# Three experts ranked by comparison, router work of a mixer tile in two slots, the next expert picked one step later, and weights split through a queue: an encoder block on one core

## The chip, the cores and the metric

The kernel runs on one core of a Trainium2 chip. The metric is the device time of one execution in microseconds, as the median of three runs. The engines of the core are TensorE (PE: matmuls and transposes), VectorE (DVE), ScalarE (ACT), GpSimd (POOL) and SyncE (SP, which here only issues transfers). Each works through its own queue in order, and semaphores make one wait for another.

## The reference

One layer of an encoder on 1024 tokens of width 1024, in float32: a token mixer and then a mixture of experts in which each expert picks its tokens.

```python
p = jnp.einsum('bsd,dk->bsk', modulate(rms_norm(x, g_norm_mix), shift_m, scale_m), w_in)
z = gate_a * (fourier_mix(u_f) @ w_fourier) + gate_b * ((b_g * centred_conv3(c_g * v)) @ w_conv_out)
x = x + gate_m * (z @ w_o)
h = modulate(rms_norm(x, g_norm_moe), shift_f, scale_f)
# expert_choice_moe(h), 16 experts, cap = 2 * 1024 / 16 = 128 tokens each
probs = softmax(h @ w_router + b_router)
vals, idx = lax.top_k(jnp.swapaxes(probs, 1, 2), cap)      # per expert: its 128 tokens
xe = h[idx]
a, u = xe @ w_gate_e, xe @ w_up_e                          # 1024 -> 2048, per expert
y = (silu(a) * u) @ w_down_e                               # 2048 -> 1024
x = x + gate_f * scatter_add(y * vals)
return rms_norm(x, g_final)
```

## The kernel before

**The stages.** A mixer (0 to about 757 us), whose last part, `mix_out`, goes over eight tiles of 128 tokens: z @ w_o, the residual, the norm, the router's logits and its softmax. Then the router's end and the first gather (to about 777 us), then the 16 experts one after the other (to about 1930 us), and the last expert's rows, which leave by a scattered transfer.

**Precision.** Weights and activations are float32. Each is split into a high and a low part: ACT copies the high part (rounded) and DVE subtracts it (`split`, L92 and L93). A product is then three matmuls: high x high, high x low and low x high. For a weight matrix of an expert the parts are called whi and wlo; for the expert's tokens xh and xl; for the product h = silu(a) * u, transposed, hth and htl.

**An expert.** Its weights are 24 units of 1 MB, each two halves of 1024 columns. A half costs ACT one copy (whi), DVE one subtraction (wlo) and PE six matmuls of 512 columns. Six buffers of whi and six of wlo are there (`NWB`), and a ring of twelve units of raw weights ahead of them, which SP fills. The 2048 inner columns go in four parts, fc 0 to 3, of 512. For each part `expert` computes a (four halves), u (four halves) and, for the part before, y (four halves). `put(fc)` transposes h of a part with four PE transposes (L1205), and ACT and DVE make hth and htl of them. During fc 1, `pick` finds the next expert's tokens: DVE compares each token's place with the slots (oh, L1068), PE multiplies it by the table (L1075), DVE reads r, idx and val from that, and POOL gathers the rows (xg). `turn` transposes xg at the end of the expert (L1104). The expert's result is scaled into ys (L1269) and added to the tokens in memory; the code puts this addition off into the next expert (`self.left`).

**The last expert** has some of its halves multiplied without a split (`plain`, L1222, with htf, the unsplit transposed h), while ACT and DVE norm the finished rows of the other tokens (`final`, `FIN` says where they are loaded).

**Choosing tokens.** An expert takes the 128 tokens with the highest probability. For experts 0 and 1 (`NCMP` = 2), `compare` ranks the tokens during `mix_out`: DVE compares each token's probability with that of all tokens of earlier tiles (cmp) and of its own tile (own), and PE counts (L972). For the other 14, `router` searches the threshold in steps during the first experts (mask, cand, ok, base).

**Order.** A scheduler orders each engine's queue from the order in which the code is written, from priorities and from dependencies. `issue_after` pins one instruction behind another. Within `mix_out`, `side(n)` puts the previous tile's router work ahead of k-step n of the present tile's eight.

Of the kernel before, what the change touches and what calls it, by code (L numbers as in the profile page):

```python
# [15 lines left out]
P = 128  # L16
D = 1024
# [12 lines left out]
NCMP = 2  # L30
FIN = ((10, 0), (8, 2), (6, 4), (4, 6))
# [49 lines left out]
class Block:  # L81
# [578 lines left out]
    def rstd(self, pool, ss, name):  # L660
        nc = self.nc
        n = ss.shape[1]
        ms = pool.tile([P, n], F32, name=name + "ms")
        nc.vector.tensor_scalar(ms, ss, 1.0 / D, EPS, op0=OP.mult, op1=OP.add)
        rs = pool.tile([P, n], F32, name=name + "rs", bufs=2)
        nc.gpsimd.tensor_tensor(rs, ms, self.neghalf[:, 0:n], op=OP.pow)
        return rs
# [66 lines left out]
    def mix_out(self, pool):  # L734
# [91 lines left out]
        def side(n):  # L826

            t, x2, rs = prev
            if t == 0 and n in (1, 5):
                next(rw, None)  # L830
            if n == 1 and t:
                hold["cmp"] = self.compare(t - 1, range(NCMP), psum)
                next(hold["cmp"])
            if n == 3:
                if t:
                    next(hold["cmp"], None)
                hold["xt"] = turned()
                for hf in range(2):
                    turn(x2, hold["xt"], hf)
            if n == 6:  # L840
                pl = psum()
                for hf in range(2):
                    logits(pl, hold["xt"], hf)
                softmax(t, rs, pl)

        prev, hold = None, {}
        for t in range(ST):
# [37 lines left out]
            for n in range(2):  # L885
                cs = slice(512 * n, 512 * n + 512)
                for k in range(KD):
                    s = {(0, 1): 1, (0, 4): 3, (1, 0): 6}.get((n, k))
                    if s:
                        side(s)  # L890
                    if n == 1 and k == 4:
# [43 lines left out]
    def compare(self, t, es, psum):  # L935
# [12 lines left out]
        num = pc[:, 256:256 + 8 * ne].rearrange("p (e t) -> p e t", e=ne)  # L948
# [12 lines left out]
        for i, e in enumerate(es):  # L961
            own = pool.tile([P, P], BF16, name="own", bufs=2)
# [3 lines left out]
            if last:  # L966
                own = pool.tile([P, P], BF16, name="own", bufs=2)
# [87 lines left out]
    def route_rest(self, pool):  # L1055
        yield from self.compare(ST - 1, (1,), self.psum)
# [82 lines left out]
    def plain(self, rows):  # L1139

        raw = self.take().rearrange("p (i k n) -> p i k n", i=2, k=rows // 2)
        for i in range(2):
            yield raw[:, i]
            if i:
                self.fetch()
            self.step()

    def unit(self, rows):

        raw = self.take()  # L1150
        nc = self.nc
        for i in range(2):
            hi = self.wsp.tile([P, 1024], F32R, name="whi")
            lo = self.wsp.tile([P, 1024], F32R, name="wlo")
            src = raw[:, 1024 * i:1024 * i + 1024]
# [7 lines left out]
            else:  # L1163
                self.split(hi, lo, src)
            self.npop += 1
            if i:
                if self.npop <= NWS:
                    with self.tc.issue_after(self.gather):
                        self.fetch(nc.gpsimd)
                else:  # L1170
                    self.fetch()
            self.pin = self.last
            self.step()
            yield hi.rearrange("p (k n) -> p k n", k=rows // 2), lo.rearrange("p (k n) -> p k n", k=rows // 2)

    def expert(self, pool, e, picked, side):
# [8 lines left out]
        def up(fc, name):  # L1185
            ps = self.pau.tile([P, 512], F32, name=name)
            k = 0
            for b in range(2):
                for j, (wh, wl) in enumerate(self.unit(4)):
                    if self.npop > NWB and (j == 0 or self.ranked < 2):  # L1190
# [5 lines left out]
                if self.left:  # L1196
                    self.left.pop()()
            return ps

        def put(fc):  # L1200
# [6 lines left out]
            if last and fc in (1, 2):  # L1207
                hf = pool.tile([P, 4, P], F32, name="htf")
# [9 lines left out]
        def down(fc, b):  # L1218
            if last and (fc, b) in ((1, 1), (2, 0), (2, 1)):
                for i, w in enumerate(self.plain(2)):  # L1220
                    for n in (0, 512):
                        nc.tensor.matmul(y[:, n:n + 512], lhsT=ht[fc][2][:, 2 * b + i, :], rhs=w[:, 0, n:n + 512],  # L1222
                                         start=False, stop=False)
                return
            for i, (wh, wl) in enumerate(self.unit(2)):
# [7 lines left out]
        for fc in range(4):  # L1233
            pa = up(fc, "a")
            if last and fc == 0:
# [28 lines left out]
        if not last:  # L1264
            down(3, 1)

            def add():
                ys = pool.tile([P, D], F32, name="ys")
                nc.vector.scalar_tensor_tensor(ys, in0=y, scalar=val, in1=self.gf, op0=OP.mult, op1=OP.mult)  # L1269
                nc.gpsimd.indirect_dma_start(out=self.x2_d,  # L1270
                                             out_offset=bass.IndirectOffsetOnAxis(ap=idx[:, 0:1], axis=0),
                                             in_=ys, in_offset=None, compute_op=OP.add)
                self.scattered = e == NE - 2

            self.left.append(add)
            return nxt
        w = list(self.unit(2))
        for _ in range(8):
            self.step()
        ss = pool.tile([P, 3], F32, name="sse")  # L1280
        for n, cs in enumerate((slice(0, 512), slice(512, 768), slice(768, 1024))):
# [4 lines left out]
            nc.vector.scalar_tensor_tensor(h, in0=y[:, cs], scalar=val, in1=self.gf[:, cs], op0=OP.mult, op1=OP.mult)  # L1286
            nc.vector.tensor_tensor(xg[:, cs], xg[:, cs], h, op=OP.add)
# [36 lines left out]
    def run(self):  # L1324
# [94 lines left out]
        self.nfetch, self.npop, self.units, self.rows = 0, 0, [], []  # L1419
        def last():  # L1420
# [80 lines left out]
```

## Time and profile before

| | us |
|---|---|
| Median of 3 runs (lowest, highest) | 1948.76 (1948.51, 1949.74) |
| The profiled execution | 1944.46 |
| Its span in the trace | 1942.6 |
| PE busy (share of the span) | 1888.7 (97%) |
| DVE busy | 1583.4 (82%) |
| ACT busy | 1117.6 (58%) |

The profile is of one execution, whose time is 1.86 us more than its span, and lies 4.3 us under the median of the runs. A share of busy time says which engine the kernel cannot do without, and not where its gaps are: PE at 97% leaves some 54 us without a matmul in the whole kernel, some 15 of them in the first 50 us, 14 after 1926 us, and 13 in the steady experts between 920 and 1926 us. Transfers move 283 GB/s in the mean and are not the limit in the experts: SP's queue waits 875 us there for a buffer that DVE has yet to finish with.

### The profile page before, as it was taken

The numbers are of one execution on the slowest core, as the hardware profiler recorded it, in microseconds if no ns is written. First come the engines' busy times: TensorE is split into PE (matmuls) and PEld (weight loads), VectorE is DVE, ScalarE is ACT, GpSimd is POOL, SyncE is SP. The second block draws the span as 40 slices with busy tenths as digits, with TensorE's granted clock in tenths as the row PEclk, the third lists the DMA queues.
The fourth block names the chain that finished last, engine by engine and source line by source line (L and its number), as shares of the span: only waits on it lengthen the run. The fifth ranks groups of instructions, "written<-read, shape, count | busy, mean of one in ns | idle before, by whom it ended". The sixth has DMA issues, their size and how long they took to land.

```text
span 1942.6 us, 23945 instructions
## 1 busy us (share of the span) xinstructions
PE 1888.7 (97%) x8777; PEld 1507.7 (78%) x8777; DVE 1583.4 (82%) x2005; ACT 1117.6 (58%) x1403; POOL 136.2 (7%) x124
## 2 busy tenths in 40 slices
PE   6999999999999999999999999999999999999996
PEld 5788888777788877777888777777778778777873
DVE  5976678676853767999999898898998999989886
ACT  5533233433510433776787777777767777677764
POOL 1000000000130111000000000000000000000001
PEclk9999999999999999999999999999999999999998
DMA  8322224465774842999999999999999999999993
GB/s 298 128 67 65 87 76 154 143 228 195 232 250 140 291 180 108 396 367 346 378 372 389 354 359 376 372 364 360 392 364 355 386 366 361 380 373 355 392 367 135
DMA packets 244746, 549.02 MB, mean 283 GB/s; under 512 B 12644, under 2 KB 51652, under 8 KB 244628
## 3 DMA queue, kind: packets, MB, share of 16 engines
q1 hardware_dynamic: 229248, 494.50, 69.8%
q0 software_dynamic: 14528, 52.75, 8.6%
q8 instruction: 69, 1.13, 0.2%
q10 hardware_dynamic: 852, 0.24, 0.1%
q14 instruction: 49, 0.40, 0.1%
HBM read 507.61 MB, written 39.86 MB: 282 GB/s over the span
## 4 chain that ended last, share of the span: by engine, by line
PE 76%; DVE 12%; DMA 5%; issue 4%; ACT 2%; POOL 0%; ACTq 0%; POOLq 0%; DVEq 0%
PE pb L315 9%; DVE wlo L93 7%; PE pa L315 6%; PE pc L315 6%; PE u L1302 5%; PE u L1300 5%; PE u L1301 5%; PE y L106 5%; PE y L109 4%; PE y L112 4%; PE a L1302 4%; PE a L1301 4%; PE a L1300 4%; DMA raw<-in_w_up_e_dram 3%; PE mm L106 3%
## 5 line engine op out<-in xcount | busy, mean ns | idle before, releaser
L93 DVE TENSOR_TENSOR wlo<-raw,whi 128x1024 fp32r<-128x1024 f32 x759 | 889.0, 1218 | 61.1 <-ACT whi L92 52.5
L92 ACT ACTIVATE whi<-raw 128x1024 fp32r<-128x1024 f32 x759 | 751.4, 1052 | 61.2 <-PE y L112 21.6
L1302 PE MATMUL a<-wlo,xh 128*128 128x512 f32 x512 | 206.2, 403 | 7.0 <-DVE wlo L93 5.7
L1302 PE MATMUL u<-wlo,xh 128*128 128x512 f32 x512 | 203.6, 398 | 2.4 <-DVE wlo L93 2.4
L1300 PE MATMUL u<-whi,xh 128*128 128x512 f32 x512 | 202.5, 395 | 1.6 <-ACT whi L92 1.6
L1300 PE MATMUL a<-whi,xh 128*128 128x512 f32 x512 | 201.5, 394 | 1.9 <-ACT whi L92 1.6
L1301 PE MATMUL a<-whi,xl 128*128 128x512 f32 x512 | 201.8, 394 | 0.0
L1301 PE MATMUL u<-whi,xl 128*128 128x512 f32 x512 | 201.8, 394 | 0.0
L109 PE MATMUL y<-wlo,hth 128*128 128x512 f32 x496 | 161.3, 406 | 0.5 <-DVE wlo L93 0.3
L106 PE MATMUL y<-whi,hth 128*128 128x512 f32 x496 | 159.5, 402 | 0.0
L112 PE MATMUL y<-whi,htl 128*128 128x512 f32 x496 | 156.4, 396 | 0.0
L92 ACT ACTIVATE wh<-s 128x512 fp32r<-128x512 f32 x80 | 50.3, 631 | 135.9 <-PE pc L315 76.0
L1302 PEld LDWEIGHTS a<-wlo,xh 128*128 128x128 f32 x512 | 96.4, 188 | 39.3 <-DVE wlo L93 19.8
L1302 PEld LDWEIGHTS u<-wlo,xh 128*128 128x128 f32 x512 | 96.3, 188 | 31.1 <-DVE wlo L93 8.0
L1300 PEld LDWEIGHTS a<-whi,xh 128*128 128x128 f32 x512 | 96.7, 189 | 21.9 <-ACT whi L92 2.5
L1301 PEld LDWEIGHTS a<-whi,xl 128*128 128x128 f32 x512 | 96.5, 188 | 22.0 <-DVE xl L93 0.4
L1300 PEld LDWEIGHTS u<-whi,xh 128*128 128x128 f32 x512 | 96.5, 188 | 21.0 <-ACT whi L92 2.6
L1301 PEld LDWEIGHTS u<-whi,xl 128*128 128x128 f32 x512 | 96.6, 189 | 20.5
L112 PEld LDWEIGHTS y<-whi,htl 128*128 128x128 f32 x496 | 93.4, 189 | 22.5
L106 PEld LDWEIGHTS y<-whi,hth 128*128 128x128 f32 x496 | 91.8, 189 | 20.9 <-issue 0.5
L109 PEld LDWEIGHTS y<-wlo,hth 128*128 128x128 f32 x496 | 89.9, 190 | 20.4 <-DVE wlo L93 2.4
L1243 ACT ACTIVATE h<-a 128x512 f32<-128x512 f32 x64 | 38.2, 596 | 106.6 <-PE a L1302 106.6
(530 smaller groups left out, 3183.1 us busy)
## 6 DMA issues: line engine op xcount, KB each, us to landing
raw<-in_w_gate_e_dram SPq DMA_DIRECT2D x126, 1024.0 KB, 7.2
raw<-in_w_up_e_dram SPq DMA_DIRECT2D x126, 1024.0 KB, 9.1
raw<-in_w_down_e_dram SPq DMA_DIRECT2D x126, 1024.0 KB, 8.1
ld<-in_w_ada_dram SPq DMA_DIRECT2D x48, 512.0 KB, 5.4
ld<-in_w_in_dram SPq DMA_DIRECT2D x44, 512.0 KB, 4.4
sg_d<-q POOLq DMA_DIRECT2D x8, 1024.0 KB, 6.1
ld<-sg_d SPq DMA_DIRECT2D x16, 512.0 KB, 4.9
x<-in_x_dram SPq DMA_DIRECT2D x8, 512.0 KB, 3.3
```

Of the source, the lines that this page charges most:

```text
L92: a = self.nc.scalar.activation(hi, src, AF.Copy).ins
L93: self.last = a, self.nc.vector.tensor_tensor(lo, src, hi, op=OP.subtract).ins
L106: nc.tensor.matmul(o, lhsT=lh, rhs=rh, start=first, stop=False)
L109: nc.tensor.matmul(o, lhsT=lh, rhs=rl, start=False, stop=False)
L112: nc.tensor.matmul(o, lhsT=ll, rhs=rh, start=False, stop=last)
L315: nc.tensor.matmul(o, lhsT=x[:, k, :], rhs=y[:, k, :], start=first and k == 0 and i == 0, stop=last and k == 3 and i == 2, skip_group_chec ...
L1243: nc.scalar.activation(h, pa, AF.Silu)
L1300: nc.tensor.matmul(o, lhsT=lhs[0], rhs=rhs[0], start=first, stop=False, **kw)
L1301: nc.tensor.matmul(o, lhsT=lhs[1], rhs=rhs[0], start=False, stop=False, **kw)
L1302: nc.tensor.matmul(o, lhsT=lhs[0], rhs=rhs[1], start=False, stop=last, **kw)
```

## The change

It does seven things. (1) `NCMP` is 3: one more expert is ranked by comparison, the search is for 13 experts. (2) The router work of a mixer tile is issued at two k-steps, 2 and 6, instead of 1, 3 and 6 (for tile 0 at 1, 3, 5 and 6), and the counting half of `compare` follows the softmax; in the last tile the places change likewise. (3) The next expert is picked in fc 2 (`PICK`) and no longer in fc 1. (4) Weight halves go through a queue: `half` issues the split of one half, and `unit` fills the queue up to six halves before it hands one to the matmuls. The order in which units come is written in a list, `plan`; `free` asks for the next transfer. (5) silu(a) is issued right behind a, and ys right behind the expert's last part. (6) htf has two buffers, and the final rows are loaded at other places (`FIN`). (7) At the end one multiplication by the final gain stands behind the first operation of `rstd`, with the order pinned.

```diff
-NCMP = 2
-FIN = ((10, 0), (8, 2), (6, 4), (4, 6))
+NCMP = 3
+PICK = 2
+FIN = ((8, 0), (7, 2), (5, 4), (4, 6))
+PLAIN = ((1, 1), (2, 0), (2, 1))
...
-            if t == 0 and n in (1, 5):
-                next(rw, None)
-            if n == 1 and t:
-                hold["cmp"] = self.compare(t - 1, range(NCMP), psum)
-                next(hold["cmp"])
-            if n == 3:
-                if t:
-                    next(hold["cmp"], None)
+            if n == 2:
+                if t == 0:
+                    next(rw, None)
                 hold["xt"] = turned()
                 for hf in range(2):
                     turn(x2, hold["xt"], hf)
+                if t:
+                    hold["cmp"] = self.compare(t - 1, range(NCMP), psum)
+                    next(hold["cmp"])
             if n == 6:
...
                 softmax(t, rs, pl)
+                if t:
+                    next(hold["cmp"], None)
...
-                    s = {(0, 1): 1, (0, 4): 3, (1, 0): 6}.get((n, k))
+                    s = {(0, 4): 2, (1, 1): 6}.get((n, k))
...
+        self.queue.append([x.rearrange("p (k n) -> p k n", k=rows // 2) for x in parts])
...
+    def unit(self):
+
+        for i in range(2):
+            while len(self.queue) < NWB and self.nunit < len(self.plan):
+                self.half()
+            self.nused += 1
+            yield self.queue.pop(0)
...
-                hf = pool.tile([P, 4, P], F32, name="htf")
+                hf = pool.tile([P, 4, P], F32, name="htf", bufs=2)
...
             pa = up(fc, "a")
+            h = pool.tile([P, 512], F32, name="h", bufs=2)
+            nc.scalar.activation(h, pa, AF.Silu)
...
             pu = up(fc, "u")
-            h = pool.tile([P, 512], F32, name="h", bufs=2)
-            nc.scalar.activation(h, pa, AF.Silu)
             nc.vector.tensor_tensor(h, pu, h, op=OP.mult)
             hs[fc] = h
-            if fc == 1:
+            if fc == PICK:
...
-            nc.vector.tensor_tensor(xg[:, cs], xg[:, cs], self.gl[:, cs], op=OP.mult)
+            if n < 2:
+                with tc.issue_after(order):
+                    order = nc.vector.tensor_tensor(xg[:, cs], xg[:, cs], self.gl[:, cs], op=OP.mult).ins
...
-        rs = self.rstd(pool, st, "e")
+        rs, order = self.rstd(pool, st, "e", True)
+        with tc.issue_after(order):
+            nc.vector.tensor_tensor(xg[:, cs], xg[:, cs], self.gl[:, cs], op=OP.mult)
```

What the scheduler makes of it is seen in the engines' queues. Line numbers of the changed program differ: its split is L94 and L95, its put L1222.

PE's queue where u of fc 2 ends in an expert in the middle of the run, before:

```order
L1302 MATMUL u<-wlo,xh 128x512
L106 MATMUL y<-whi,hth 128x512 x2
L109 MATMUL y<-wlo,hth 128x512 x2
L112 MATMUL y<-whi,htl 128x512 x2
L106 MATMUL y<-whi,hth 128x512 x2
L1205 MATMUL tp<-ident,h 128x128 x4
```

and of the change, at the same place:

```order
L1323 MATMUL u<-wlo,xh 128x512
L108 MATMUL y<-whi,hth 128x512 x2
L111 MATMUL y<-wlo,hth 128x512 x2
L114 MATMUL y<-whi,htl 128x512 x2
L108 MATMUL y<-whi,hth 128x512 x2
L111 MATMUL y<-wlo,hth 128x512 x2
L114 MATMUL y<-whi,htl 128x512 x2
L108 MATMUL y<-whi,hth 128x512 x2
L1222 MATMUL tp<-ident,h 128x128 x4
```

The four transposes of h have moved from 8 to 14 matmuls behind the end of u. ACT's queue in the same expert, from the h of fc 0 to the hth of fc 2, before:

```order
L1243 ACTIVATE h<-a 128x512
L92 ACTIVATE whi<-raw 128x1024 x6
L92 ACTIVATE hth<-tp 128x512
L92 ACTIVATE whi<-raw 128x1024 x2
L1243 ACTIVATE h<-a 128x512
L92 ACTIVATE whi<-raw 128x1024 x8
L92 ACTIVATE hth<-tp 128x512
L92 ACTIVATE whi<-raw 128x1024 x4
L1243 ACTIVATE h<-a 128x512
L92 ACTIVATE whi<-raw 128x1024 x6
L92 ACTIVATE hth<-tp 128x512
```

and of the change:

```order
L1254 ACTIVATE h<-a 128x512
L94 ACTIVATE whi<-raw 128x1024 x6
L94 ACTIVATE hth<-tp 128x512
L94 ACTIVATE whi<-raw 128x1024 x2
L1254 ACTIVATE h<-a 128x512
L94 ACTIVATE whi<-raw 128x1024 x6
L94 ACTIVATE hth<-tp 128x512
L94 ACTIVATE whi<-raw 128x1024 x6
L1254 ACTIVATE h<-a 128x512
L94 ACTIVATE whi<-raw 128x1024 x6
L94 ACTIVATE hth<-tp 128x512
```

The hth of fc 1 (the second of the three) now has six copies ahead of it, as the others have, and had eight. In the tail, PE's queue where u of fc 2 of the last expert ends, before:

```order
L1302 MATMUL u<-wlo,xh 128x512
L1205 MATMUL tp<-ident,h 128x128 x4
L106 MATMUL y<-whi,hth 128x512 x2
L109 MATMUL y<-wlo,hth 128x512 x2
L112 MATMUL y<-whi,htl 128x512 x2
L106 MATMUL y<-whi,hth 128x512 x2
L109 MATMUL y<-wlo,hth 128x512 x2
L112 MATMUL y<-whi,htl 128x512 x2
L1222 MATMUL y<-raw,htf 128x512 x4
L1300 MATMUL a<-whi,xh 128x512
```

and of the change:

```order
L1323 MATMUL u<-wlo,xh 128x512
L108 MATMUL y<-whi,hth 128x512 x2
L111 MATMUL y<-wlo,hth 128x512 x2
L114 MATMUL y<-whi,htl 128x512 x2
L108 MATMUL y<-whi,hth 128x512 x2
L111 MATMUL y<-wlo,hth 128x512 x2
L114 MATMUL y<-whi,htl 128x512 x2
L1239 MATMUL y<-raw,htf 128x512 x4
L1222 MATMUL tp<-ident,h 128x128 x4
L1321 MATMUL a<-whi,xh 128x512
```

The transposes stand behind the matmuls without a split (L1222 before, L1239 in the change) and no longer ahead of the part y.

## Rows read from the trace of the kernel before

Times of the timeline are from the start of the span: start, duration, engine, line, operation, tiles, count; in brackets what the engine waited before it.

**Rows 1.** The page's groups by line: engine, tiles, count, busy, mean ns, idle before.

```profile
L93 DVE TENSOR_TENSOR wlo<-raw,whi 128x1024 fp32r<-128x1024 f32 x759 | 889.0, 1218 | 61.1 <-ACT whi L92 52.5
L92 ACT ACTIVATE whi<-raw 128x1024 fp32r<-128x1024 f32 x759 | 751.4, 1052 | 61.2 <-PE y L112 21.6
```

**Rows 2.** Busy time by stretches: length, PE, PEld, DVE, ACT, POOL, PEclk, DMA, GB/s.

```profile
777.00:895.00 118.00, 115.41 (x622) 89.59 (x621) 115.50 (x185) 87.74 (x91) 3.71 (x2) 1.00 1.02 380
880.00:900.00 20.00, 17.16 (x85) 12.91 (x84) 19.93 (x36) 11.19 (x12) 1.13 (x1) 0.87 0.94 351
920.00:1926.00 1006.00, 992.61 (x4486) 790.60 (x4485) 902.21 (x884) 731.22 (x825) 55.92 (x33) 1.00 1.00 365
...
1340.00:1360.00 20.00, 19.57 (x90) 15.55 (x89) 18.30 (x18) 14.65 (x18) 2.32 (x1) 1.00 0.97 322
1898.00:1902.00 4.00, 3.90 (x11) 2.60 (x10) 3.59 (x5) 3.23 (x5) 0.31 (x1) 0.57 0.87 351
```

**Rows 3.** Timeline of PE behind ys in expert 8.

```profile
1353.19 0.39 PE L1301 MATMUL a<-whi,xl 128*128 128x512 f32 x1
1354.01 0.50 PE L1302 MATMUL a<-wlo,xh 128*128 128x512 f32 x1 [0.43 <-DVE wlo L93]
```

**Rows 4.** Timeline of PE and DVE at the pick in expert 8.

```profile
1368.35 0.36 PE L1075 MATMUL tp<-v,oh 128*128 128x5 bf16 x8
...
1371.18 0.40 PE L1301 MATMUL u<-whi,xl 128*128 128x512 f32 x1
1371.75 0.50 PE L1302 MATMUL u<-wlo,xh 128*128 128x512 f32 x1 [0.18 <-DVE wlo L93]
...
1369.02 0.15 DVE L1077 COPY r<-tp 128x5 f32<-128x5 f32 x1
...
1370.48 2.35 DVE L93 TENSOR_TENSOR wlo<-raw,whi 128x1024 fp32r<-128x1024 f32 x2
```

**Rows 5.** Timeline of PE, ACT and DVE at two hth in expert 8.

```profile
1363.77 0.60 PE L1205 MATMUL tp<-ident,h 128*128 128x128 f32 x4
...
1364.40 0.60 ACT L92 ACTIVATE hth<-tp 128x512 fp32r<-128x512 f32 x1 [1.50 <-PE tp L1205]
...
1380.56 0.27 PE L1205 MATMUL tp<-ident,h 128*128 128x128 f32 x1
...
1383.20 0.40 PE L1301 MATMUL a<-whi,xl 128*128 128x512 f32 x1
1383.72 0.51 PE L1302 MATMUL a<-wlo,xh 128*128 128x512 f32 x1
...
1380.87 0.60 ACT L92 ACTIVATE hth<-tp 128x512 fp32r<-128x512 f32 x1 [4.60 <-PE tp L1205]
1381.36 2.94 ACT L92 ACTIVATE whi<-raw 128x1024 fp32r<-128x1024 f32 x3
...
1382.44 2.36 DVE L93 TENSOR_TENSOR wlo<-raw,whi 128x1024 fp32r<-128x1024 f32 x2 [0.25 <-ACT whi L92]
```

**Rows 6.** PE's waits in the whole span: total us, times, longest.

```profile
PE sm L972 <- DVE cmp L958: 2.5, 6, 0.6
```

**Rows 7.** Timeline of DVE at the end of the mixer's last tile.

```profile
755.63 1.14 DVE L958 TENSOR_SCALAR_CACHE_REDUCE cmp<-prow,prob 128x896 bf16<-128x896 f32 x1
...
757.63 0.69 DVE L804 TENSOR_TENSOR ld<-mm,ld 128x512 f32<-128x512 f32 x1
```

**Rows 8.** Timeline of PE at the pick of expert 2.

```profile
895.75 0.38 PE L1075 MATMUL tp<-v,oh 128*128 128x5 bf16 x8 [2.85 <-DVE oh L1068]
```

**Rows 9.** Timeline of ACT and PE in the last expert.

```profile
1894.77 0.60 ACT L1209 ACTIVATE htf<-tp 128x512 f32<-128x512 f32 x1 [7.00 <-PE y L1222]
...
1896.36 0.50 PE L1300 MATMUL a<-whi,xh 128*128 128x512 f32 x1 [1.63 <-ACT whi L92]
...
1906.43 0.50 PE L1300 MATMUL u<-whi,xh 128*128 128x512 f32 x1 [1.63 <-ACT whi L92]
```

**Rows 10.** Timeline of DVE behind the last y.

```profile
1931.99 0.42 DVE L1289 TENSOR_TENSOR xg<-xg,ys 128x256 f32<-128x256 f32 x1 [0.63 <-ACT h L1288]
```

More of the change, by code (lines that the diff above doesn't have):

```diff
@@ L961, in compare @@
         for i, e in enumerate(es):
-            own = pool.tile([P, P], BF16, name="own", bufs=2)
+            own = pool.tile([P, P], BF16, name="own")
             r = row[:, i, :] if last else self.prow[:, e, n:n + P]
@@ L1055, in route_rest @@
     def route_rest(self, pool):
-        yield from self.compare(ST - 1, (1,), self.psum)
+        yield from self.compare(ST - 1, range(1, NCMP), self.psum)
         self.ranked = NCMP
@@ L1137, in step, with half @@
                 next(r, None)
[L1139 to L1150, printed above, removed]
-        nc = self.nc
-        for i in range(2):
+    def half(self):
+        nc = self.nc
+        rows, plain = self.plan[self.nunit]
+        i = self.nhalf
+        if i == 0:
+            self.raw = self.take()
+        src = self.raw[:, 1024 * i:1024 * i + 1024]
+        if plain:
+            parts = [src]
+        else:
             hi = self.wsp.tile([P, 1024], F32R, name="whi")
             lo = self.wsp.tile([P, 1024], F32R, name="wlo")
-            src = raw[:, 1024 * i:1024 * i + 1024]
+            parts = [hi, lo]
             if self.npop < NWS:
@@ L1164, in unit, with free @@
                 self.split(hi, lo, src)
+                self.pin = self.last
             self.npop += 1
[L1166 to L1174, printed above, removed]
+        self.queue.append([x.rearrange("p (k n) -> p k n", k=rows // 2) for x in parts])
+        if i:
+            if not plain:
+                self.free(self.nunit)
+            self.nunit += 1
+        self.nhalf = 1 - i
+        self.step()
+    def free(self, n):
+        self.read.add(n)
+        while self.nfree in self.read:
+            self.nfree += 1
+            if self.nfree == 1:
+                with self.tc.issue_after(self.gather):
+                    self.fetch(self.nc.gpsimd)
+            else:
+                self.fetch()
+    def unit(self):
[4 more added lines that the diff above has]
+            yield self.queue.pop(0)
     def expert(self, pool, e, picked, side):
@@ L1218, in down @@
         def down(fc, b):
-            if last and (fc, b) in ((1, 1), (2, 0), (2, 1)):
-                for i, w in enumerate(self.plain(2)):
+            if last and (fc, b) in PLAIN:
+                for i, (w,) in enumerate(self.unit()):
                     for n in (0, 512):
@@ L1419, in run @@
         self.nfetch, self.npop, self.units, self.rows = 0, 0, [], []
+        self.plan = []
+        for e in range(NE):
+            for f in range(5):
+                self.plan += [(4, False)] * (4 if f < 4 else 0)
+                self.plan += [(2, e == NE - 1 and (f - 1, b) in PLAIN) for b in range(2 if f else 0)]
+        self.nunit, self.nhalf, self.nfree, self.nused, self.queue, self.read = 0, 0, 0, 0, [], set()
         def last():
@@ L1474, in run @@
         self.hold = self.turned
-        self.left = []
         for e in range(NE):
```

45 lines of the change are left out of this document (23 added, 22 removed).

## Prediction

> **What bounds the kernel now.** I first read the busy time by stretches. TensorE (PE) is busy 992.61 of the 1006 us from 920 to 1926, at a granted clock of 1.00, while DVE has 902.21 and ACT 731.22 [rows 2]. So in the experts the time is the sum of PE's own work, and a change is worth what it adds to or takes from PE's gaps. The groups by line give the price of a half: ACT copies it to whi in 1052 ns, DVE makes wlo in 1218 ns [rows 1]; PE takes six matmuls about 0.23 us apart, 1.385 us. Both helpers are faster than PE, and there are six buffers of each, so in the mean PE need not wait. It waits where ACT or DVE has to stop for something that PE itself does late.
>
> The timelines show three such places in each of the experts 5 to 13, every 71.02 us. (1) Behind ys, a DVE instruction: starts at 1353.19 and 1354.01 where 0.23 is usual, a loss of 0.59 (11 times) [rows 3]. (2) Behind r, idx, val, oh: DVE is off the wlo from 1369.02 to 1370.48, and PE's starts are 1371.18 and 1371.75: 0.34 lost (9 times) [rows 4]. (3) Behind hth of fc 1, the place to understand [rows 5]. The last transpose starts at 1380.56; only 0.31 later can ACT copy it, at 1380.87; the next whi starts at 1381.36, its wlo at 1382.44, and PE reads that at 1383.72. PE had wanted it at 1383.20 + 0.23: lost 0.29 (9 times, and 0.63 once in expert 4). So 1.22 us per expert, about 13 in all. Note that ACT had been idle 4.60 before that hth: it stood in its queue ahead of the whi that it could have made.
>
> **Lead** is what I call the halves that ACT has issued ahead of hth, less those that PE has finished when the transposes start. At (3) it is 1.67 (h of the second matrix's a has lead 2; eight whi follow it in ACT's order; PE does four halves of u, four of y and two matmuls). For the other hth of before it is 2.67 (six whi, four halves of u and eight matmuls: 2 + 6 - 5.33), and there PE has no gap: transposes at 1363.77, hth at 1364.40, and the next matmul with wlo on time [rows 5].
>
> **Steady experts.** The new code writes the splits ahead of the matmuls that need them, and the program's order shows what this does: six whi still stand between h and hth, but the transposes come 14 matmuls behind u instead of 8. The lead becomes 2 + 6 - 6.33 = 1.67 in fc 0, 1 and 2 (2.0 in fc 3). The price follows from the rows just read. With T0 the start of four transposes: hth at T0 + 0.63 (1363.77 to 1364.40), from hth to PE 2.85 (1380.87 to 1383.72), so T0 + 3.48. PE wants it after the transposes (0.35), ten matmuls of finished halves and two that need whi only: 0.35 + 12 x 0.23 = T0 + 3.10, or 3.14 in y. Loss 0.38 and 0.34 at fc 0 and fc 2, where before has none.
>
> At fc 1 the pick of the next expert now stands two wlo behind that htl, where before it stood behind the htl of fc 0. Two wlo start at T0 + 2.20 and end their turn at T0 + 4.50 (2 x 1.15), r to oh takes 1.46 [rows 4], to T0 + 5.96, and the next wlo reaches PE 1.28 later (1382.44 to 1383.72), T0 + 7.24. PE wants it four halves on: 0.35 + 5.54 + 0.12, and 0.22 for the eight oh matmuls (0.36 from first start to last end [rows 4], less the overlap with the next), T0 + 6.23. Loss 1.01, the hth's own part in it. The ys keeps its lead of two halves, so 0.59 stays; that ys is issued at once and not in the next expert changes nothing in DVE's order here, as wlo of the queue stand ahead of it.
>
> Per expert: 0.59 + 0.38 + 1.01 + 0.34 = 2.32 against 1.22, +1.10; ten experts (4 to 13) +11.0. Expert 14 picks nothing: about +0.8. Expert 15 loses 0.38 and 0.34 and, at fc 1, has htf and hth both ahead of the whi, about 0.5 more: +1.2. Together **+13**. Bounds: +4 if a lead of 1.67 costs nothing where the transposes fall inside y, and only the pick costs; +21 if each hth costs 0.63 as the one in expert 4 did.
>
> **Mixer.** PE waits 2.5 us in 6 places at L972 for the compare [rows 6]; from start to start the gaps there are some 4 us. The second half of compare now comes behind softmax, four k-steps later, so DVE's cmp (0.6 to 1.1 us each) is done: -4.0. The third expert adds seven transposes and 21 small matmuls on PE, +1.8 at 0.05 for each of the small ones and some 0.1 for each transpose. In the last tile DVE's order has a third cmp and own ahead of the add to ld; a cmp of 896 columns takes 1.14, and that add started at 757.63 with PE idle for it [rows 7]. The two cost 1.4, some 0.4 of it was slack (the place and cnt additions are moved behind): +1.0. Sum **-1.1**, bounds -2.5 and +1.
>
> **First experts.** From 777 to 895 DVE is full, 115.5 of 118 us [rows 2]: it makes wlo and runs the search for the 14 other experts. At the end PE stands 2.85 us, until 895.75, for the oh of expert 2 [rows 8], loses 1.15 more right after, and the granted clock is 0.87 in 880 to 900, some 2 us more. The change makes the search narrower (416 instead of 448 columns, some 7% of mask, ok and cand, -0.7 of DVE time) and adds cmp and own for a third expert (+2); and oh(2) is again placed with five halves more of DVE work ahead of it than PE has had: I count 4.6 us of DVE work beyond PE's in both orders. So the stall stays: **+0.3**, bounds -6 (stall, its follow-on and the slow clock all go: 2.85 + 1.15 + 2) and +2.
>
> **The tail.** In the last expert ACT is held 7.00 us at htf, whose one buffer the plain matmuls still read, until 1894.77, and PE's a starts 1.63 late, at 1896.36; the same happens at u, 1906.43 [rows 9], and the clock falls to 0.57 in 1898 to 1902 [rows 2]. The second htf buffer removes that wait, but the order now puts the transposes behind the eight plain matmuls, and the htf waits for them with no lead: they start at 6.22 after the end of u (2.8 for twelve matmuls, 3.4 for the plain ones), a starts at 8.44 where it was 9.74. The u that follows loses its wait, but DVE's scaling of final rows (1.28) and a wlo per half, 2.4 us, set its pace. I take u's end 1.8 us earlier. At the very end two multiplies by gl (0.42, row 1931.99 [rows 10]) leave the chain behind y, less what the pinned order costs: -0.5. Sum **-2.3**, bounds -0.5 and -3.5.
>
> **Sum.** 13.0 - 1.1 + 0.3 - 2.3 = +9.9 on the profiled execution's 1944.46, so 1954.4; that execution lies 4.3 us under the median 1948.76, so a median of 1958.7, say **1958.5**.
>
> **Rivals.**
> - *The stall at 895 goes.* If oh(2) is made a few wlo earlier relative to PE, up to 6 us return; 9.9 - 6.3 = +3.6, 1952: within the noise (0.2%, about 3.9 us, is what a measurement of this kernel can tell from no change). For it: the search is 7% narrower. Against: DVE's total there rises.
> - *Faster: hth does not hold the whi.* Place: hth at fc 0, 1, 2. If ACT and DVE are far enough ahead that hth and oh cost nothing in the new order (the gaps of (2) and (3) then vanish too, 0.63 x 10), the sum is -6.3 - 1.1 + 0.3 - 2.3 = -9.4: 1939.4. With L the loss at hth and pick in an expert (forecast 1.73, before 0.63) the kernel comes out equal at about L = 0.75 and faster by 0.2% below 0.35. For it: the transposes come later, so PE no longer can wait for h, and DVE's h has a lead of 2 halves instead of 1. Against: (3) has just this lead and loses.
> - *Slower still: the gaps drop the clock.* Two of the clock's levels stand in the trace, 1.00 (2.4 GHz) and stretches toward half. After the 2.85 us stop before 895.75 it was low for about 2 us of loss. A pick's stall of 1 us in ten experts would, at that price, give +20: 1978. Against: the 0.59 stall lies in 1340 to 1360, with 1.00 granted and 19.57 of 20 busy [rows 2]. The Trainium skill, page "TensorE: Matmul & The Clock Gate", section "HAM oscillation — how this bites in real kernels", says that a wait recurring in every tile can halve the clock again each time; by that rule this rival would come true. This trace agrees with it only for the long stops (0.87 around 895, 0.57 after 1896), not for the short ones.
>
> **Numbers.** The forecast (more gaps in the experts than the ends give back) 0.62, its own range 1952.7 to 1967; the rival at 895, or smaller steady losses of that size, 0.15; faster 0.17; the clock 0.06. The range must leave out no more than 2 in 10: from 1943 (most of the faster case below it) to 1967 (steady losses at 0.5 per hth). Faster by over 0.2%: 0.17; within: 0.14; slower: 0.69.
>
> **What would show it.** Right: in every expert three hth with ACT idle before them and, 2.85 us on, a matmul with wlo that starts 0.3 to 0.4 late, at fc 1 one of about 1 us behind oh; a period near 72.1 us instead of 71.02; no wait at the small matmuls of compare; htf without a 7 us wait. Wrong: a period of 71 us or less; no idle PE behind hth; an oh(2) that comes before PE asks for it; or granted clocks under 1.00 within the steady experts.

## The result, and the profile after

The changed kernel takes 1975.24 us (median; 1972.43 to 1979.42) against 1948.8: 1.0137 times as long, with a 95% interval of 1.0115 to 1.0158. Slower was forecast, by 10 us; it is 26.4. The profiled execution took 1972.43, 28.0 more than that of before. The page after, the lines of the span, PE, DVE and the clock:

```profile
span 1970.7 us, 24079 instructions
PE 1909.6 (97%) x8813; PEld 1517.9 (77%) x8813; DVE 1591.2 (81%) x2040; ACT 1116.8 (57%) x1403; POOL 133.9 (7%) x124
...
PEclk9999999999999998999999999999999999999998
```

PE is busy 20.9 us longer (1888.7 before), in a program with 36 more matmuls, most of them tiny. That alone says that much of the loss is not gaps. Where it lies is found by landmarks that both programs have: the first matmul of z @ w_o, the transposes of the gathered tokens of experts 0, 5 and 15, and the last 512-column matmul of y. PE's timeline before:

```profile
638.40 0.74 PE L106 MATMUL mm<-woh,zh 128*128 128x512 f32 x2 [1.07 <-ACT zh L92]
774.44 0.74 PE L1104 MATMUL tp<-ident,xg 128*128 128x128 f32 x5 [0.75 <-DMA xg<-h_d,idx]
1131.21 0.60 PE L1104 MATMUL tp<-ident,xg 128*128 128x128 f32 x4
1840.40 0.60 PE L1104 MATMUL tp<-ident,xg 128*128 128x128 f32 x4
1926.30 0.49 PE L1302 MATMUL y<-wlo,hth 128*128 128x512 f32 x1
```

and after:

```profile
638.75 0.50 PE L108 MATMUL mm<-woh,zh 128*128 128x512 f32 x1 [1.07 <-ACT zh L94]
782.79 0.41 PE L1108 MATMUL tp<-ident,xg 128*128 128x128 f32 x2 [1.20 <-DMA xg<-h_d,idx]
1142.02 0.60 PE L1108 MATMUL tp<-ident,xg 128*128 128x128 f32 x4
1866.81 0.38 PE L1108 MATMUL tp<-ident,xg 128*128 128x128 f32 x2
1953.13 0.49 PE L1323 MATMUL y<-wlo,hth 128*128 128x512 f32 x1
```

| stretch, us | before | after | difference | forecast |
|---|---|---|---|---|
| to the first z @ w_o | 638.40 | 638.75 | +0.35 | 0 |
| mixer: z @ w_o to expert 0's tokens | 136.04 | 144.04 | +8.00 | -1.1 |
| experts 0 to 4 | 356.77 | 359.23 | +2.46 | +1.4 |
| experts 5 to 14 | 709.19 | 724.79 | +15.60 | +10.7 |
| expert 15 to the last full y | 85.90 | 86.32 | +0.42 | -0.6 |
| end | 16.30 | 17.57 | +1.27 | -0.5 |

**The steady expert.** Its period, from one expert's tokens to the next one's, is 72.57 where it was 71.02. PE's timeline in expert 9 shows the stalls, in this order: behind ys; behind hth of fc 0; behind the pick; behind hth of fc 2.

```profile
1441.36 0.40 PE L1322 MATMUL a<-whi,xl 128*128 128x512 f32 x1
1442.15 0.50 PE L1323 MATMUL a<-wlo,xh 128*128 128x512 f32 x1 [0.39 <-DVE wlo L95]
...
1456.51 0.40 PE L1322 MATMUL u<-whi,xl 128*128 128x512 f32 x1
1456.99 0.50 PE L1323 MATMUL u<-wlo,xh 128*128 128x512 f32 x1
...
1471.65 0.40 PE L1322 MATMUL a<-whi,xl 128*128 128x512 f32 x1
1472.72 0.50 PE L1323 MATMUL a<-wlo,xh 128*128 128x512 f32 x1 [0.67 <-DVE wlo L95]
...
1487.02 0.39 PE L1322 MATMUL a<-whi,xl 128*128 128x512 f32 x1
1487.52 0.50 PE L1323 MATMUL a<-wlo,xh 128*128 128x512 f32 x1
```

Each pair's distance from start to start, less the usual 0.23, is the loss: 0.56, 0.25, 0.84, 0.27, together 1.92, where [rows 3 to 5] give 1.22. That accounts for 0.70 of the 1.55. The rest is not in any gap. The groups by line, of a stretch from 1432 to 1800, show it in the mean of one matmul; before and then after:

```profile
L1300 PE MATMUL u<-whi,xh 128*128 128x512 f32 x169 | 66.2, 392 | 0.0
```

```profile
L1321 PE MATMUL u<-whi,xh 128*128 128x512 f32 x160 | 63.4, 396 | 0.0
```

The same instruction takes 4 ns longer. From start to start (mean over all expert matmuls that follow one another without a wait) a and u take 0.2340 us, where before they take 0.2297, in each of the 16 experts; y takes 0.2326, where before it takes 0.2331. 192 matmuls of a and u x 0.0043 are 0.83 us per expert.

**The mixer.** The granted clock by stretches (its column is the third from the end):

```profile
655.00:670.00 15.00, 15.00 (x79) 12.85 (x78) 7.81 (x21) 6.09 (x11) 1.58 (x3) 0.89 1.00 315
745.00:757.00 12.00, 10.78 (x63) 8.70 (x62) 8.33 (x26) 2.01 (x7) 0.56 (x1) 0.86 0.12 48
757.00:766.00 9.00, 7.41 (x56) 6.66 (x55) 6.40 (x18) 2.24 (x6) 0.00 (x0) 0.77 0.15 60
766.00:776.00 10.00, 10.00 (x70) 9.99 (x69) 6.91 (x21) 6.13 (x9) 0.55 (x1) 0.69 0.29 105
```

Before, it is 1.00 throughout. In tile 0 PE waits for nothing ahead of the fall. Its timeline there:

```profile
659.65 1.86 PE L798 MATMUL sm<-wsf,ones 128*128 128x16 f32 x16
661.36 0.26 PE L756 MATMUL sm<-wr,hth 128*128 128x32 f32 x1
...
663.12 0.36 PE L758 MATMUL sm<-wr,htl 128*128 128x16 f32 x1
663.34 1.20 PE L108 MATMUL mm<-woh,zh 128*128 128x512 f32 x2
664.33 1.05 PE L111 MATMUL mm<-wol,zh 128*128 128x512 f32 x2
665.19 1.05 PE L114 MATMUL mm<-woh,zl 128*128 128x512 f32 x2
```

Thirty-two matmuls of 16 and 32 columns stand in a row, which the slots of before kept in two groups; behind them two matmuls of 512 columns take 0.86 where two take 0.46 elsewhere. PE's timeline in the last tile:

```profile
750.43 0.67 PE L976 MATMUL sm<-onesb,cmp 128*128 128x1 bf16 x10
751.70 0.80 PE L108 MATMUL mm<-woh,zh 128*128 128x512 f32 x1 [0.59 <-DVE ld L806]
752.29 0.63 PE L111 MATMUL mm<-wol,zh 128*128 128x512 f32 x1
752.72 0.63 PE L114 MATMUL mm<-woh,zl 128*128 128x512 f32 x1
...
762.76 0.32 PE L976 MATMUL sm<-onesb,cmp 128*128 128x1 bf16 x6 [1.43 <-DVE cmp L962]
762.94 1.63 PE L660 MATMUL mm<-ident 128*128 128x128 f32 x6
```

From 748.31 to 751 PE did only matmuls of 1 to 32 columns, then waited 0.59 for DVE. The next 512-column matmuls start 0.59 and then 0.43 apart, where such a matmul takes some 0.23 at 2.4 GHz: this is the lower of the two levels, 1.2 GHz. Later it waits 1.43 for the third cmp.

### The profile page after: what moved, and what is told of

Same layout as the page of the kernel before. It is cut to its first block, busy times and chain, and to the rows that moved or that the text cites. A ratio compares the mean times of both kernels' runs of the same rounds, so it can differ in the third digit from the quotient of the medians.

```text
span 1970.7 us, 24079 instructions
## 1 busy us (share of the span) xinstructions
PE 1909.6 (97%) x8813; PEld 1517.9 (77%) x8813; DVE 1591.2 (81%) x2040; ACT 1116.8 (57%) x1403; POOL 133.9 (7%) x124
## 4 chain that ended last, share of the span: by engine, by line
PE 70%; DVE 12%; DMA 10%; issue 4%; ACT 4%; POOL 1%; POOLq 0%; DVEq 0%; ACTq 0%; SPq 0%
PE pb L317 8%; DVE wlo L95 8%; PE pa L317 6%; PE pc L317 6%; PE a L1323 5%; DMA raw<-in_w_gate_e_dram 4%; PE u L1322 4%; PE u L1321 4%; PE u L1323 4%; PE a L1322 4%; PE a L1321 4%; ACT whi L94 3%; PE mm L108 3%; PE mm L114 3%; DMA raw<-in_w_up_e_dram 3%
## 5 line engine op out<-in xcount | busy, mean ns | idle before, releaser
L95 DVE TENSOR_TENSOR wlo<-raw,whi 128x1024 fp32r<-128x1024 f32 x759 | 888.8, 1218 | 68.1 <-ACT whi L94 66.1
L94 ACT ACTIVATE whi<-raw 128x1024 fp32r<-128x1024 f32 x759 | 751.8, 1052 | 61.5 <-PE y L114 23.6
L94 ACT ACTIVATE wh<-s 128x512 fp32r<-128x512 f32 x80 | 50.4, 632 | 135.7 <-PE pc L317 71.6
L94 ACT ACTIVATE hth<-tp 128x512 fp32r<-128x512 f32 x63 | 37.6, 596 | 146.5 <-PE tp L1222 146.5
```

The costliest lines, as they stand in the source:

```text
L94: a = self.nc.scalar.activation(hi, src, AF.Copy).ins
L95: self.last = a, self.nc.vector.tensor_tensor(lo, src, hi, op=OP.subtract).ins
```

## The experiments

Execution times scatter by several us on some chips (the kernel before: 1942 to 1957 in the later groups of runs), and the first z @ w_o starts anywhere from 638 to 648 in programs that are alike up to there. So stretches between the landmarks are compared, and ratios serve for the total.

### Where xh lies

The sizes of prow, own, place and pad decide at which byte of a partition the tiles behind them start. In the built programs xh starts at byte 102048 before and at 105536 in the change; whi and wlo stay where they were, each of their buffers 224 over a multiple of 256. Below, 'a and u' and 'y' with a figure stand for the mean time of such a matmul from start to start (the step), and 'over' for the rest of a tile's first byte within 256 if nothing else is said. The first pair adds a filler:

```diff
         self.gf = mp.tile([P, D], F32, name="gf")
+        self.pad = mp.tile([P, 8], F32, name="pad")
+        nc.gpsimd.memset(self.pad, 0.0)
```

> The kernel before with one unused tile of 32 bytes per partition ahead of xh, so that xh, xl, h, hth, htl and ys lie 32 bytes further on (xh at byte 102080 in place of 102048; the change has it at 105536); nothing else. In the change each a or u matmul takes 0.2340 us from start to start where before it takes 0.2297. Theory 'place': the place of the tokens' tiles decides, by their start in units of 64 bytes (before 32 over, change 0 over): then this kernel has a step near 0.234, and 192 x 16 x 0.0043 = 13 us more, some 1962. Rival 'order': the step belongs to the change's instruction order: then this kernel stays at 0.2297 and 1949. Third: it is the place, but not in units of 64 (the distance to other tiles): 0.2297 and 1949 too, and the next kernel tells.

> The changed kernel with the same 32 bytes ahead of xh (byte 105568). Theory 'place': a and u matmuls go back to 0.2297 us, some 13 us less than the change's 1975, so 1962. Rival 'order': 0.2340 and 1975 as in the change.

Measured: the kernel before with 32 bytes more takes 1.0032 times its time (1.0013 to 1.0051), a and u 0.2332, period 71.45; the change with 32 more takes 1.0104 (1.0086 to 1.0122), a and u 0.2325, period 72.39. The first shows that the place decides: its instructions stand as before. What was expected of the second failed: the step did not go back to 0.2297. The filler in the next two is 32 and 24 words of four bytes, on the kernel before and on the change:

> The kernel before with an unused tile of 128 bytes ahead of xh (xh at byte 102176). With 32 bytes the same program took 0.2332 us for each a or u matmul in place of 0.2297, and 6 us more. Theory 'residue': what counts is where xh starts within 128 bytes (32 over before, 64 over with 32 bytes more and in the change, 96 over in the change with 32 more). Here it is 32 over again: 0.2297 and the time of before, within 2 us. Rival 'distance': only the exact old place is fast: 0.2325 to 0.2340, 6 us or more.

> The changed kernel with 96 bytes ahead of xh (byte 105632, 32 over within 128, as before). 'Residue': a and u at 0.2297 us, the period of an expert 72.57 down by some 0.5 to 0.7 (slower matmuls gave DVE time, so the stalls grow a little when they get faster), 7 to 10 us in all: 1965 to 1968. Rival 'distance': 0.2325 to 0.2340 and 1970 to 1975.

The first took 1.0041 (1.0024 to 1.0058) with a step of 0.2332, so 'residue within 128' falls. The second took 1.0082 (1.0054 to 1.0111) with 0.2297 and a period of 71.99: 9 us less than the change itself, by 96 bytes. Both have xh 32 over within 128, but only the second has it 160 over within 256, as the kernel before. Two single executions more, with 16 and 24 words on the kernel before:

> The kernel before with 64 bytes ahead of xh: xh 224 over within 256, hth 64 over. So far a and u took 0.2297 us with xh 160 over (three kernels), 0.2332 at 32 and 192, 0.2340 at 64, 0.2325 at 96. By 'residue within 256' any value of 0.2297 to 0.2340 can come, but the same at each expert; y, with hth 64 over, stays at 0.2325 to 0.2333. Rival 'distance': one value at 160 is chance, and the next kernel with 160 over breaks it (the one put together above has 160 at another byte).

> The kernel before with 96 bytes ahead of xh: xh 0 over within 256, hth 96 over. By 'residue' a and u between 0.2297 and 0.2340, y at 0.2325 as in the change, which also has hth 96 over; 'distance' says nothing of y.

With xh 224 over, a and u take 0.2281 (period 70.87, less than before); with 0 over 0.2331 (71.36). Their totals, 1953.35 and 1954.99, say nothing by themselves: z @ w_o began 9.5 and 3.4 us later than in the profile of before. The groups by line, from 1432 to 1800, of the kernel before with 32 bytes, with 64 bytes, and of the change with 96 bytes:

```profile
L1300 PE MATMUL u<-whi,xh 128*128 128x512 f32 x164 | 64.8, 395 | 0.0
```

```profile
L1300 PE MATMUL u<-whi,xh 128*128 128x512 f32 x168 | 65.6, 390 | 0.0
```

```profile
L1321 PE MATMUL u<-whi,xh 128*128 128x512 f32 x160 | 62.8, 392 | 0.0
```

All readings by the start of the stationary tile within 256 bytes: 0: 0.2331; 32: 0.2332; 64: 0.2340; 96: 0.2325; 128: 0.2333 (hth in y); 160: 0.2290 to 0.2306; 192: 0.2332; 224: 0.2275 to 0.2283. They come from 17 programs; where several have one residue, at other bytes, they agree within 0.0016, and xh and hth agree at the same residue. Since whi and wlo lie 224 over in all 17, a place counted from theirs (the same place, or 64 bytes below it, would be the good ones) fits as well as one within 256; no run tells the two apart.

### The lead of hth, and the pick

```diff
-PICK = 2
+PICK = 1
```

> The changed kernel with the next expert picked in fc 1 again. In the change PE loses 0.84 behind the pick in each expert (period 72.57). Theory 'queue': the pick's place costs 0.84 - 0.34, and hth of fc 1 gets its lead of 1.67 from eight copies as before: period 72.1 to 72.4, 3 to 5 us less, 1971. Rival: the pick only meets another stall there and the period stays at 72.57 or grows, 1975 or more.

1.0118 (1.0093 to 1.0144) and a period of 72.57: the rival was right. The pick's stall moved with it into u of fc 1 and kept its 0.84. The place of the pick is not the cause.

```diff
+                pin = b == 0 and i == 1 and fc < 3
+                if pin:
+                    put(fc + 1)
+                with after(self.turns if pin else None):
                   self.mm3([y[:, 0:512], y[:, 512:1024]], [t[:, 2 * b + i, :] for t in ht[fc][0:2]],
...
-            pa = up(fc, "a")
+            pa = up(fc, "a", (lambda: put(0)) if fc == 1 else None)
```

> The changed kernel with the four transposes of h pinned six matmuls behind the end of u (14 in the change), so that hth stands with a lead of 3.0 halves in ACT's queue at fc 0, 1 and 2 and of 3.0 at fc 3; the pick stays in fc 2. Theory 'lead': the stalls behind hth (0.25 at fc 0, 0.27 at fc 2, each with 0.1 more for the restart) go, and that behind the pick shrinks from 0.84 to below 0.4 as the halves ahead of it are earlier: the period falls from 72.57 to between 71.4 and 71.9, 8 to 13 us less: 1963 to 1968. Rival: PE waits for h at the earlier place (DVE makes it behind two wlo), the stall only moves: 72.4 or more.

1.0061 (1.0044 to 1.0078); the period is 71.60, 0.97 less, at the same slow step (0.2340). ACT's timeline at fc 0, 1 and 2:

```profile
1451.77 0.60 ACT L94 ACTIVATE hth<-tp 128x512 fp32r<-128x512 f32 x1 [1.27 <-PE tp L1229]
...
1463.55 0.60 ACT L94 ACTIVATE hth<-tp 128x512 fp32r<-128x512 f32 x1 [1.27 <-PE tp L1229]
...
1481.56 0.60 ACT L94 ACTIVATE hth<-tp 128x512 fp32r<-128x512 f32 x1 [1.80 <-PE tp L1229]
```

ACT still waits, and PE does not: the losses behind hth of fc 0 and 2 are gone, and the pick costs 0.05. Only the 0.50 behind ys is left. In the first experts, with leads of 5 to 6 in both kernels, PE lost more instead (experts 0 to 4 took 362.8, against 359.23 at the same slow step); the cause of that stays open. Of the 14.5 us by which this kernel's median is below the change's, 8.1 lie in the last expert, which was not expected: from expert 15's tokens to the last full y it takes 78.26 where the change takes 86.32. There the transposes of fc 2 stand ahead of the plain matmuls again, htf is ready at 1910.75, before the plain ones start at 1911.35, and PE's a follows them at 1914.38 without a wait.

### The mixer

The old slots in the change:

```diff
-            if n == 2:
...
+            if t == 0 and n in (1, 5):
+                next(rw, None)
+            if n == 1 and t:
+                hold["cmp"] = self.compare(t - 1, range(NCMP), psum)
+                next(hold["cmp"])
+            if n == 3:
...
```

> The changed kernel with the router work of a mixer tile in the slots of before (1, 3, 6, and the last tile's), all else as in the change, so three experts are compared there too. In the change the first expert's tokens are turned at 782.79, before at 774.44: 8.35 us, of which 3.66 by the last matmul of the mixer and 4.69 behind it, with a granted clock of 0.69 to 0.86 there. Theory 'slots': putting the logits' and the compare's small matmuls together makes the clock fall and the wait for ld: undone, the clock is 1.00 there and the time falls by 5 to 8, to 1968. Rival 'third expert': the third compare costs it: then less than 2 us return, 1974.

The clock is 1.00 throughout, and the stretch takes 140.37, 3.7 less than in the change's profile, but the time is 1.0123 (1.0102 to 1.0143): the mixer gives back, an earlier part of that execution lost it (z @ w_o began at 645.78). In other kernels with the change's own mixer the stretch took 141.1 to 144.7, so the old slots are worth 1 to 4 us here. The same with two experts:

```diff
-NCMP = 3
+NCMP = 2
```

> The changed kernel with the slots of before and two experts compared: only the queue, the pick in fc 2 and the tail are changed; xh lies at byte 101792 (32 over within 128). From the first matmul of z @ w_o to the turn of the first expert's tokens: before 136.0 us, change 144.0, change with the old slots 140.4. Theory 'third expert': 136 to 137 here. Rival 'queue': the fetches and splits that the queue issues there cost it: 139 or more. By 'residue' a and u take 0.2297. Total by theory: 1962 to 1964 (period some 72.0: +11, tail +2).

1.0044 (1.0027 to 1.0061), a and u 0.2297. The stretch took 142.67, not 136: the clock was at 0.50 from 668 to 676, in tile 0, behind sixteen matmuls of 16 columns and a wait of 0.77 for DVE's htl. Neither theory is settled by it. The two kernels at the end, with the same slots, queue and two experts, took 137.7 and 138.1. New slots with two experts, and the old end chain:

```diff
-            with tc.issue_after(order):
-                nc.vector.scalar_tensor_tensor(h, in0=y[:, cs], scalar=val, in1=self.gf[:, cs], op0=OP.mult,
-                                               op1=OP.mult)
+            nc.vector.scalar_tensor_tensor(h, in0=y[:, cs], scalar=val, in1=self.gf[:, cs], op0=OP.mult, op1=OP.mult)
...
```

> The changed kernel with two experts compared and the end chain of before; slots, queue, pick and tail as in the change; xh 160 over within 256. Two places are read. Mixer, from the first matmul of z @ w_o to the turn of the first expert's tokens: before 136.0 to 137.1, old slots with three experts 140.4, new slots with three 141.1 to 144.7. Theory 'third expert costs 4.4 and the slots little but for the clock': 136.5 to 138 where the clock stays, up to 140 where it falls. Rival 'slots': 140 or more at a granted clock of 1.00. End, from the last full-width y matmul to the span's end: before 16.07, change 17.34. Theory 'pin' (h of y stands behind a multiplication that waits for ACT's square): 16.0 to 16.3. Rival: 17 or more, it is the clock. The period of an expert 71.97.

1.0066 (1.0049 to 1.0083). The mixer took 141.5 with the clock falling at both places, so fewer experts do not keep it up. From the last full y the end took 16.27, as before (16.30; 17.57 in the change): that the change's end chain costs 1.3 is shown. In the change's tail, DVE and PE:

```profile
1955.93 0.69 DVE L1308 TENSOR_TENSOR xg<-xg,ys 128x512 f32<-128x512 f32 x1 [0.79 <-ACT h L1305]
1956.54 0.48 DVE L1302 SCALAR_TENSOR_TENSOR h<-y,val,gf 128x256 f32<-128x256 f32 x1
...
1957.07 0.58 PE L1321 MATMUL y<-whi,hth 128*128 128x256 f32 x1 [1.63 <-DVE h L1302]
```

The scaling of y that PE waits for is pinned behind a multiplication that itself waits 0.79 for ACT's square; PE waits 1.63 where it waited 0.58 (and 0.58 in the kernel with the old end chain). The last two take one part alone on the kernel before: the slots (the first), and the third expert with a filler that keeps xh at 160 over.

> The kernel before with the mixer's router work in the change's two slots, and nothing else (two experts, the split and pick of before, xh 160 over). From the first matmul of z @ w_o to the first expert's turn: before 136.0 to 137.9 in five profiles, new slots with two experts and the queue 141.5 at a granted clock that fell twice (0.83 in three stretches of ten us). Theory 'slots with the clock': 139 to 142 with falls in tile 0 and the last tile; 1951 to 1954. Rival 'slots only together with the queue's splits': 136 to 138 with the clock at 1.00, and 1949 or less.

1.001 (0.9997 to 1.0024). In the profile the stretch took 135.5, less than before, although the clock fell in the last tile:

```profile
750.00:760.00 10.00, 9.90 (x51) 8.14 (x51) 4.97 (x15) 2.00 (x6) 0.00 (x0) 0.83 0.00 1
```

So the waits at L972 [rows 6] do go (0.2 us is left of 2.5), which is worth about 1.2 in the loop of z @ w_o (117.12 for 118.28), and the clock takes some of it back. In tile 0 the same block of small matmuls as in the change left the clock at 1.00; PE's timeline there:

```profile
663.20 1.85 PE L796 MATMUL sm<-wsf,ones 128*128 128x16 f32 x16
...
666.69 0.71 PE L106 MATMUL mm<-woh,zh 128*128 128x512 f32 x2
667.25 0.62 PE L109 MATMUL mm<-wol,zh 128*128 128x512 f32 x2
```

The times of this kernel reach from 1946.9 to 1957.5.

> The kernel before with three experts compared, in the old slots, with xh kept 160 over within 256 by a filler. Theory 'third expert': the same stretch takes 140 to 141 (as with the change's queue and old slots, 140.4), 2.7 of it in the loop, 1.7 behind its last matmul, at a clock of 1.00; 1952 to 1954, as the first experts' search gets a little shorter. Rival: the queue's part in it, 137 to 138 here and 1949.

0.9998 (0.9985 to 1.0011). The stretch took 139.96 at a clock of 1.00: the third expert costs 3.9 against the profile of before, and 2 to 4 against the five profiles of that mixer (136.0 to 138.0). But the forecast of the total failed; PE's timeline at the tokens of experts 1 and 2:

```profile
856.26 0.93 PE L1104 MATMUL tp<-ident,xg 128*128 128x128 f32 x7
929.42 0.82 PE L1104 MATMUL tp<-ident,xg 128*128 128x128 f32 x6
```

That interval is 73.16, and it was 78.87 before: the stall of [rows 8] is gone, with the slow clock behind it. Experts 0 to 4 take 3.7 us less than before, and so a third expert pays for itself in this order. In the change it does not: a stall of the same kind stands in expert 0 instead, 1.77 us for a mask at 852.42, with 512-column matmuls 0.43 apart behind it.

### Put together

The change's queue and tail, two experts, old slots, old end chain, transposes pinned from expert 3 on, and xh and hth at 160 over; then both at 224 over.

> A kernel put together from what the runs showed: the change's queue, pick in fc 2 and tail, but two experts compared, the mixer slots of before, the end chain of before (no pinned order), the transposes of h pinned six matmuls behind u from the fourth expert on, xh at a byte 160 over within 256 (as in the three kernels that took 0.2297 us), and hth moved there too (it lay 0 over). By 'lead': only ys and a small rest stall, so with a step of 0.2297 the period is 70.9 to 71.1 (71.60 with 0.2340); the tail from the last expert's turn to the end 94 to 96 in place of 102.2; mixer as before. Sum 1938 to 1944, if the place of hth changes nothing in y (0.2332); if it does as for xh, 96 x 0.0035 = 0.3 us less per expert, 5 us less in all. Rival: the stalls only move, or the mixer's start loses as much as in the other kernels with the queue (2 to 4 us): 1946 to 1950.

> The kernel put together from the runs (1938.6), with xh and hth 224 over within 256 in place of 160. The one run with xh there took 0.2281 us for a and u where 160 takes 0.2295. By 'residue' a, u and y take 0.2275 to 0.2282; of the 0.4 us per expert that this is worth, stalls behind ys and the pick take back half: 2 to 5 us less, 1934 to 1937. Rival: DVE is what bounds the expert by now, and the time stays within 1.5 us of 1938.6.

The first took 1938.61, 0.9958 (0.9943 to 0.9973) of the time before; y takes 0.2290 there with hth at 160, where it takes 0.2325 to 0.2340 elsewhere. Its period is 71.03: matmuls faster by 1.2 us per expert than in the kernel with pinned transposes (192 x 0.0046 and 96 x 0.0039) gave 0.57, since the stalls grow where PE comes sooner. The tail from expert 15's tokens to the end is 94.3 (102.2 before). That is most of what it gains, 7.8 us where the medians differ by 9.5; in experts 5 to 14 it gains nothing (710.1, 709.2 before), although its matmuls are a little faster. The second took 1933.81, 0.9918 (0.9898 to 0.9937): a and u 0.2278, y 0.2275, period 70.77. It is faster than the kernel before and than the change.

## Why the prediction was wrong

**Steady experts: the mechanism was right, and the stalls nearly so.** The loss at hth of fc 0 and 2 was put at 0.38 and 0.34 and measured 0.25 and 0.27; the pick at 1.01, measured 0.84; ys at 0.59, 0.56. Pinning the transposes removed all but ys, as the lead says. With xh back at 160 over, the period is 71.99 (near 72.1 forecast) and experts 5 to 14 take 718.95, 9.8 more than before, where 10.7 was forecast. The part that the forecast gave to the pick's new place is wrong: with the pick in fc 1 again the stall stayed, and with the larger lead it went.

**The step that failed** is the sentence that "a change is worth what it adds to or takes from PE's gaps". It held PE's own work for fixed. The third expert's rows in the tiles ahead of xh (prow above all) moved it from 160 to 64 over within 256 bytes (with two experts, and all else of the queue, it lies 160 over again), and each a and u matmul became 4.3 ns longer: 5.8 us in experts 5 to 14 (724.79 less 718.95), 2.0 in 0 to 4 (359.23 less 357.27), 0.5 in the last. That is 8.3 of the 16.5 by which the difference of the medians (26.4) is above the forecast's 9.9.

**The mixer's term** was put at -1.1 and is +8.0 in the profile (5 to 9 in the other kernels with the change's mixer). The gain at L972 was taken as 4.0 and is 1.2 in the loop; a wait of 1.43 for the third cmp stays. The third expert was put at 1.8 of PE work and 1.0 behind the loop, and costs 3.9 in its profile (the loop 3.3 longer, the rest behind it), 2 to 4 with the scatter of the others; in it PE waits 2.9 us for cmp, 1.0 for ld and 0.9 for htl (2.5, 0.2 and 0.5 before), so part of that price is DVE's. The change's loop is as long as that kernel's (121.59 and 121.55); its other 4.0 us lie behind the loop, where the clock is at 0.69 and 0.77. How much of them the clock alone takes is not measured. The clock fell in all seven profiles with the new slots (six of the change's kind, one with the slots alone) and in two of the ten with the old slots: in tile 0 of the one with the queue and two experts, and in the first ten us of the fastest kernel. So it goes with the new slots, but what makes it fall is not settled. In tile 0 of the change thirty-two small matmuls without a wait stood ahead of it, and in the kernel with the slots alone the same block left it at 1.00; in the last tile of these two, small matmuls and a wait of 0.59 and of 0.50 stood ahead; and without the new slots sixteen small matmuls and a wait of 0.77 did it once.

**The first experts** came near the forecast (+0.5 without the place, 1.4 forecast), but by luck: the forecast kept the stall at the pick of expert 2, and there it is gone (70.58 from expert 1's tokens to expert 2's, 78.87 before), as one of its rivals said. In its place the search stalls expert 0, which takes 78.64 where it took 71.45.

**The tail.** a starts 8.45 behind u (8.44 forecast), u ends 26.8 behind it (26.35). The end was forecast at -0.5 and is +1.27: the change's end chain with its pinned order, whose cost I took to be small, costs 1.3, as shown. ACT's wait at htf, whose end I gave as a sign [rows 9], is still there, now for the transposes behind the eight plain matmuls, and whi is split after it, so PE's a still waits 1.63 and then 0.52 for wlo. ACT and PE after:

```profile
1921.69 0.60 ACT L1226 ACTIVATE htf<-tp 128x512 f32<-128x512 f32 x1 [7.89 <-PE tp L1222]
...
1923.29 0.50 PE L1321 MATMUL a<-whi,xh 128*128 128x512 f32 x1 [1.63 <-ACT whi L94]
```

**The rival of the clock** in the experts did not come: a stall of 0.84 recurs in each, and 1432 to 1505 has a granted clock of 1.00. In the mixer the clock did fall, behind waits that were no longer and once behind none. The Trainium skill (page "TensorE: Matmul & The Clock Gate", section "HAM oscillation — how this bites in real kernels") tells of a kernel in which the wait of each tile halves the clock again; its waits are far longer than the stalls of these experts, so the forecast was wrong to say that this rule makes the rival come true, and the trace, with 1.00, does not speak against it.

## What to carry to other kernels

Count how many pieces of work a helper has issued ahead of an instruction that waits for the bound engine, less those that this engine will have used by then: a helper that is fast in the mean stalls the bound engine if that lead is too small (here 1.67 halves stalled it, 2.67 and 3.0 did not), and a few instructions' shift decides it. When a change alters the size of any tile, compare the mean time of the untouched matmuls before looking for gaps; a filler of some bytes is the test. Pin an order only where nothing that is pinned ahead waits for another engine.

## What was not expected of the hardware

A float32 matmul with a 128x128 stationary tile and 512 columns took 0.2275 to 0.2340 us from start to start, and which of these depends on where the stationary tile (xh and xl, or hth and htl, which move together) starts within 256 bytes, best at 224 and 160; measured on 16 experts in each of 17 programs, for xh and for hth. Why those two is open, and so is whether the place counts by itself or from that of whi and wlo, which was the same throughout; only the eight multiples of 32 were tried. The Trainium skill, page "SBUF — State Buffer", section "Operand start alignment", asks of a start only that it be a multiple of the element size, and says that its runs timed nothing: all places here keep that rule, and some 8 us of this kernel's time lie between two of them.
